# A decoder layer on one Trainium2 core: stick-breaking attention ahead of the banded attention, its branch merged second, and plain gates in the merge for the DeltaNet branch alone

## The chip, the core and the metric

The kernel runs on one core of one Trainium2 chip. A core has five engines with a queue each: TensorE (PE, matmuls and transposes), VectorE (DVE), ScalarE (ACT), GpSimd (POOL) and SyncE (SP, which here issues DMAs). An engine takes its instructions in order; across engines they wait on semaphores. The metric is the device time of one execution in microseconds.

## The reference, cut to what matters

One layer of a hybrid decoder over 512 tokens of width 2048. The part that the change touches is the mixer: three branches on the same input, each multiplied by its own sigmoid gate and summed.

```python
def hybrid_mixer(xn, w_in, ..., w_br_dn, w_br_swa, w_br_sb, w_o):
    proj = xn @ w_in
    ...
    o_dn = gated_delta_rule(q, k, v, g, beta)
    ...
    y_swa = sliding_window_gqa(...)      # banded: 8 heads of 64, window 128, ALiBi, sinks
    y_sb = stick_breaking_attention(...) # 4 heads of 128
    gate = jax.nn.sigmoid(gates).reshape(bsz, seq, N_BRANCH, D_MODEL)
    merged = gate[:, :, 0] * (y_dn @ w_br_dn) + gate[:, :, 1] * (y_swa @ w_br_swa) + gate[:, :, 2] * (y_sb @ w_br_sb)
    return merged @ w_o
```

Before it stands an RMSNorm; behind it follow a cross-attention, a convolutional FFN and a last norm, which the change leaves alone.

## The kernel before

All activations lie transposed: a tile is 128 channels by 512 tokens. Products keep float32 accuracy by splitting each operand into a rounded part (`h`, `wh`) and a remainder (`l`, `wl`); three matmuls replace one. `dense` (lines 151 to 170) computes a 128 x 512 output tile so: it loads 512 KB of weights at a time into `raw` (three buffers), ACT casts them to `wh` (line 163), DVE forms `wl` (line 164), each with two buffers used in the order in which the program asks for them, and PE runs three matmuls for each of 16 pieces of the inner dimension: 48 in all (lines 168 to 170).

The stages, in the program's order:

1. Input norm and transposes; `xh`, `xl` are the split input.
2. Gates. There are 16 column tiles (`m`) for each of three branches (0 DeltaNet, 1 banded, 2 stick-breaking). `strassen_pair` computes two of them in seven half-size products (56 pairs of a 512 wide and a 256 wide matmul; line 366 is the first of each). For `m` from `MP` = 2 on, all three branches' gates go this way, through the sigmoid and to DRAM; then the DeltaNet values (four more pairs).
3. DeltaNet (region `p_dn`).
4. Region `p_b`: the banded attention, then the stick-breaking attention.
5. Merge (region `p_c`): for each `m` and each branch, the gate (for `m` < 2 by `dense`, otherwise read from DRAM into `sg`), then the branch's product with its weights, then gate times product, summed into `mrg[m]`. At `m` = 0 the branch inputs `y` are split into `yh` and `yl`; these tiles lie in the region's memory, which the region before it used.
6. Output projection and the rest.

The banded attention projects K and V (one `dense` each), and then for each of four head pairs a Q tile. A pair's 512 queries go in four blocks. A block is a chain: scores on PE (line 750, two heads), bias on DVE (756), row maximum (760) and small operations, exponentials on ACT (765, 767), normalisation on DVE (769 to 771), transposes on PE (774), a copy on ACT (776), the product with the values on PE (779). The first block of a pair has 128 keys a head, the others 256. A stick-breaking head projects V, K and Q (three `dense` tiles), and then has one chain over all keys (lines 797 to 845).

Each engine's order is made when the program is built: a scheduler places each instruction by its priority and by when its operands and buffers are expected to be free. A weight load and its split have a raised priority. Dense matmuls of later tiles are so placed between the steps of a chain, as far as buffers for their weights and sums are to be had: `dense` sums have two PSUM buffers (`acc`), everything else in these stages six (`gps`). An engine never leaves the order made so.

The merge loop, and the order of its branches:

```python
for m in range(KT):
    for b, (w, k0, nk) in enumerate(((w_br_dn, 0, 8), (w_br_swa, 8, 4), (w_br_sb, 12, 4))):
        sg = misc.tile([P, S], F32, name="sg")
        if m < MP:
            acc = dense_ps()
            dense(acc, w_in, 0, KT, O_G + b * D + m * P, xh, xl)
            last = act.activation(sg, acc, AF.Sigmoid)
        else:
            nc.sync.dma_start(out=sg, in_=gate_d[b][m])
```

Of the kernel before, what the change touches and what calls it, by code (L numbers as in the profile page):

```python
# [9 lines left out]
F32 = mybir.dt.float32  # L10
# [3 lines left out]
AF = mybir.ActivationFunctionType  # L14
ALU = mybir.AluOpType
AX = mybir.AxisListType

P = 128
S = 512
D = 2048  # L20
KT = D // P
# [7 lines left out]
O_WQ, O_WK, O_WV = 4112, 4624, 4752  # L29
O_SQ, O_SK, O_SV, O_G = 4880, 5392, 5904, 6416  # L30
# [28 lines left out]
def decoder_kernel(ctx: ExitStack, tc: tile.TileContext, x, mem, norm_mix, w_in, dn_conv, dn_a_log, dn_dt_bias, dn_norm,  # L59
                   swa_sinks, w_br_dn, w_br_swa, w_br_sb, w_o, norm_xattn, norm_mem, w_xq, w_xkv, w_xo, norm_ffn, w_up,  # L60
                   ffn_conv, w_down, norm_final, consts, out, dbg=None):
    nc = tc.nc
    act, dve, pool, pe = nc.scalar, nc.vector, nc.gpsimd, nc.tensor
# [32 lines left out]
    def dense_ps():  # L96
        return psd.tile([P, S], F32, name="acc")

    def gen_ps():
        return gen[0].tile([P, S], F32, name="gps")  # L100
# [39 lines left out]
    def mrg_tile(k):  # L140
        return mrgp.tile([P, S], F32, name=f"mrg{k}")
# [9 lines left out]
    def dense(acc, w, r0, nk, col, hs, ls, M=P, share=False):  # L151
        for c0 in range(0, nk, 8):
            kc = min(8, nk - c0)
            raw = rawp.tile([P, 8, M], F32, name="raw")
            r = r0 + c0 * P
            with tc.high_priority(1000000):
                nc.sync.dma_start(out=raw[:, :kc, :], in_=w[r:r + kc * P, col:col + M].rearrange("(k p) c -> p k c", p=P))
            wh = wsp.tile([P, 8, M], F32R, name="wh")
            wl = wsp.tile([P, 8, M], F32R, name="wl")
            for s0 in range(0, kc, 4):  # L160
                part = slice(s0, s0 + 4)
                with tc.high_priority(1000000):
                    act.copy(wh[:, part, :], raw[:, part, :])  # L163
                    (pool if share and s0 else dve).tensor_tensor(wl[:, part, :], raw[:, part, :], wh[:, part, :].bitcast(F32),  # L164
                                                                  op=ALU.subtract)
                for j in range(s0, s0 + 4):
                    k = c0 + j
                    pe.matmul(acc, wh[:, j, :], hs[k], start=(k == 0), stop=False)  # L168
                    pe.matmul(acc, wh[:, j, :], ls[k], start=False, stop=False)  # L169
                    pe.matmul(acc, wl[:, j, :], hs[k], start=False, stop=(k == nk - 1))  # L170
# [18 lines left out]
    with region("p_start") as ps:  # L189
# [9 lines left out]
        pt = gen_ps()  # L199
# [137 lines left out]
    with tc.tile_pool(name="psw", bufs=2, space=bass.MemoryType.PSUM, reuse_waits="tile") as pw:  # L337
# [78 lines left out]
            act.copy(la, d[:, HT:S])  # L416
            fold(out[:, 0, HT:S], d[:, 0:HT], la)

        for m in range(MP, KT, 2):
            for b_ in range(3):  # L420
                g = gp.tile([P, 2, S], F32, name="g", bufs=1)
                strassen_pair(w_in, O_G + b_ * D + m * P, g, m == MP and b_ == 0)
                act.activation(g, g, AF.Sigmoid)
                gd = dram.tile([P, 2, S], F32, name=f"gate{b_}_{m}")
                pool.dma_start(out=gd, in_=g)
                gate_d[b_][m], gate_d[b_][m + 1] = gd[:, 0, :], gd[:, 1, :]
# [284 lines left out]
    with region("p_b") as bp:  # L711
# [9 lines left out]
        for g in range(2):  # L721
            for f in range(2):
                pool.memset(kp[g][f][64 - 64 * f:128 - 64 * f, :], 0.0)
        acc = dense_ps()
        dense(acc, w_in, 0, KT, O_WK, xh, xl)
        for g in range(2):
            for f in range(2):
                act.copy(kp[g][f][64 * f:64 * f + 64, :], acc[64 * g:64 * g + 64, :])
        acc = dense_ps()
        dense(acc, w_in, 0, KT, O_WV, xh, xl)  # L730
        vt = misc.tile([P, S], F32, name="m0")
        act.copy(vt, acc)
        pt = gen_ps()
        for t in range(4):
            pe.transpose(pt[:, t * P:(t + 1) * P], vt[:, t * P:(t + 1) * P], ident)
        wv = bp.tile([P, 4, P], F32, name="wv", bufs=1)
        dve.tensor_copy(wv, pt.rearrange("p (t c) -> p t c", t=4))
        for pr in range(4):
            acc = dense_ps()
            dense(acc, w_in, 0, KT, O_WQ + pr * P, xh, xl)  # L740
            qt = bp.tile([P, S], F32, name="wq")
            act.activation(qt, acc, AF.Copy, scale=0.125)
            g = pr // 2
            yps = gen_ps()
            for b in range(4):
                nk = 1 if b == 0 else 2
                w = nk * P
                sps = gen_ps()
                for f in range(2):
                    pe.matmul(sps[:, f * w:(f + 1) * w], qt[:, b * P:(b + 1) * P], kp[g][f][:, (b + 1) * P - w:(b + 1) * P],  # L750
                              start=True, stop=True)
                s = bp.tile([P, S], F32, name="ws")
                sv = s[:, 0:2 * w].rearrange("p (f c) -> p f c", f=2)
                for f in range(2):
                    hd = 2 * pr + f
                    dve.scalar_tensor_tensor(s[:, f * w:(f + 1) * w], dist[:, 2 * P - w:2 * P], -(2.0 ** -(hd + 1)),
                                             sps[:, f * w:(f + 1) * w], op0=ALU.mult, op1=ALU.add)
                st = bp.tile([P, 5, 2], F32, name="wst", bufs=3)
                nm, es, sm_, rr = (st[:, i, :] for i in range(4))
                dve.tensor_reduce(nm, sv, axis=AX.X, op=ALU.max)  # L760
                sk = sink[:, 2 * pr:2 * pr + 2]
                dve.tensor_tensor(nm, nm, sk, op=ALU.max)
                dve.tensor_tensor(es, sk, nm, op=ALU.subtract)
                dve.tensor_scalar(nm, nm, -1.0, None, op0=ALU.mult)
                act.activation(es, es, AF.Exp)
                for f in range(2):
                    act.activation(s[:, f * w:(f + 1) * w], s[:, f * w:(f + 1) * w], AF.Exp, bias=nm[:, f:f + 1],
                                   accum_out=sm_[:, f:f + 1])
                dve.tensor_tensor(rr, sm_, es, op=ALU.add)
                dve.reciprocal(rr, rr)  # L770
                dve.tensor_tensor(sv, sv, rr.unsqueeze(2).broadcast_to([P, 2, w]), op=ALU.mult)
                tps = gen_ps()
                for i in range(2 * nk):
                    pe.transpose(tps[:, i * P:(i + 1) * P], s[:, i * P:(i + 1) * P], ident)
                pT = bp.tile([P, S], F32, name="wpT")
                act.copy(pT[:, 0:2 * w], tps[:, 0:2 * w])
                for f in range(2):
                    for i in range(nk):
                        pe.matmul(yps[64 * f:64 * f + 64, b * P:(b + 1) * P], wv[:, b + 1 - nk + i, 64 * g:64 * g + 64],
                                  pT[:, (f * nk + i) * P:(f * nk + i + 1) * P], start=(i == 0), stop=(i == nk - 1))  # L780
            y[8 + pr] = mrg_tile(8 + pr)
            act.copy(y[8 + pr], yps)
            dbg(f"y{8 + pr}", y[8 + pr])

        wid = [S - n * P for n in range(4)]
        off = [0, 512, 896, 1152]
        for h in range(4):
# [57 lines left out]
            act.copy(y[12 + h], ops)  # L845
            dbg(f"y{12 + h}", y[12 + h])


    mrg = [None] * KT
    with region("p_c") as cp:  # L850
        yh, yl = [None] * 16, [None] * 16
        for m in range(KT):
            for b, (w, k0, nk) in enumerate(((w_br_dn, 0, 8), (w_br_swa, 8, 4), (w_br_sb, 12, 4))):
                sg = misc.tile([P, S], F32, name="sg")
                if m < MP:
                    acc = dense_ps()
                    dense(acc, w_in, 0, KT, O_G + b * D + m * P, xh, xl)
                    last = act.activation(sg, acc, AF.Sigmoid)
                else:
                    nc.sync.dma_start(out=sg, in_=gate_d[b][m])  # L860
                if m == 0:
                    for k in range(k0, k0 + nk):
                        yh[k] = cp.tile([P, S], F32R, name=f"yh{k}", bufs=1)
                        yl[k] = cp.tile([P, S], F32R, name=f"yl{k}", bufs=1)
                        split(yh[k], yl[k], y[k])
                acc = gen_ps()
                dense(acc, w, 0, nk, m * P, yh[k0:k0 + nk], yl[k0:k0 + nk])
                if b == 0:
                    mrg[m] = mrg_tile(m)
                    dve.tensor_tensor(mrg[m], acc, sg, op=ALU.mult)  # L870
                else:
                    t = misc.tile([P, S], F32, name="m0")
                    dve.tensor_tensor(t, acc, sg, op=ALU.mult)
                    pool.tensor_tensor(mrg[m], mrg[m], t, op=ALU.add)
            dbg(f"mrg{m}", mrg[m])
# [372 lines left out]
```

## Time and profile before

| what | value |
|---|---|
| time, median of 3 runs | 2842.78 us (2842.43 to 2847.3) |
| the profiled execution's own time | 2845.59 us |
| its span, first to last instruction | 2843.8 us |
| its mean granted TensorE clock | 0.997 |
| gates and DeltaNet values in pairs | 129 to 629 us |
| banded attention | about 1034 to 1145 us |
| stick-breaking attention | about 1143 to 1281 us |

How to read it: a row of the timeline gives an instruction's start, its duration, engine, line of the kernel, operation and tiles (written from read); behind it, in brackets, how long the engine had been idle and what ended that. Matmuls are pipelined, so that the distance from one start to the next is shorter than a duration. A row of the groups or of a tile gives a count and durations in nanoseconds. In the windows view each engine has its busy time and its number of instructions in the stretch, then come the granted clock of TensorE (1.00 is full), the share of the DMA engines and the bandwidth.

### The profile page before, as it was taken

To read this page: it belongs to the slowest core of one execution; us is meant where nothing else is said; L and a number is where in the kernel's file an instruction comes from. 1 tells how busy PE (TensorE), PEld (TensorE's weight loads), DVE (VectorE), ACT (ScalarE), POOL (GpSimd) and SP (SyncE) were. 2 spreads that over 40 slices of the span, in tenths; PEclk is the share of its full clock that TensorE was granted. 3 is DMA by queue.
4 is the path that set the end of the run, shared out by engine and by line. 5 is a ranking of instruction groups with operands and counts; after the bars stand their busy time and mean duration, and the time that the engine had idled before them with its cause. 6 is when DMAs were issued, how large, how long until landed. Compare 5 with 4: busy or idle time off the path is not lost. (4 is left out here: it accounts for less than half of the span.)

```text
span 2843.8 us, 40775 instructions
## 1 busy us (share of the span) xinstructions
PE 2780.3 (98%) x15959; PEld 2404.1 (85%) x15959; DVE 1852.3 (65%) x2771; ACT 1258.3 (44%) x2099; POOL 349.6 (12%) x317
## 2 busy tenths in 40 slices
PE   7999999999999999999999999999999999999998
PEld 7788888888888877778888887789999999978886
DVE  7777787877777645334554345778888888743435
ACT  6455555545434434443323334645454545532223
POOL 3100000001011000010221111311111111100002
PEclk9999999999999999999999999999999999999999
DMA  6444444443122222223555433765656565553333
GB/s 211 135 134 138 136 133 127 134 127 93 56 69 59 54 69 70 66 70 91 160 170 167 137 116 92 227 163 136 151 136 152 135 152 135 170 163 124 120 97 112
DMA packets 528467, 354.53 MB, mean 125 GB/s; under 512 B 15345, under 2 KB 483810, under 8 KB 527634
## 3 DMA queue, kind: packets, MB, share of 16 engines
q1 hardware_dynamic: 487872, 303.74, 37.4%
q0 software_dynamic: 39760, 47.93, 7.6%
q8 instruction: 125, 2.05, 0.3%
q14 instruction: 68, 0.56, 0.1%
q10 hardware_dynamic: 642, 0.26, 0.0%
HBM read 316.74 MB, written 35.13 MB: 124 GB/s over the span
## 5 line engine op out<-in xcount | busy, mean ns | idle before, releaser
L168 PE MATMUL acc<-x,wh 128*128 128x512 f32 x1152 | 456.0, 396 | 0.5 <-ACT wh L163 0.5
L164 DVE TENSOR_TENSOR wl<-raw,wh 128x512 fp32r<-128x512 f32 x394 | 287.6, 765 | 257.7 <-ACT wh L163 254.7
L169 PE MATMUL acc<-x,wh 128*128 128x512 f32 x1152 | 455.4, 395 | 0.0
L170 PE MATMUL acc<-x,wl 128*128 128x512 f32 x1152 | 455.1, 395 | 0.2 <-DVE wl L164 0.2
L163 ACT CAST wh<-raw 128x512 fp32r<-128x512 f32 x408 | 234.8, 618 | 414.7 <-PE acc L169 212.8
L170 PEld LDWEIGHTS acc<-x,wl 128*128 128x128 f32 x1152 | 217.0, 188 | 45.7 <-issue 1.6
L168 PEld LDWEIGHTS acc<-x,wh 128*128 128x128 f32 x1152 | 217.0, 188 | 44.6 <-issue 1.2
L169 PEld LDWEIGHTS acc<-x,wh 128*128 128x128 f32 x1152 | 217.2, 189 | 44.0 <-issue 2.0
L1165 DVE TENSOR_TENSOR wl<-raw,wh 128x512 fp32r<-128x512 f32 x112 | 72.4, 688 | 131.9 <-ACT wh L1164 131.9
L1030 ACT CAST wh<-sraw 128x1024 fp32r<-128x1024 f32 x87 | 91.3, 1049 | 150.0 <-PE sa L1035 97.1
L1164 ACT CAST wh<-raw 128x512 fp32r<-128x512 f32 x112 | 63.9, 618 | 178.5 <-PE gps L1171 172.2
L1030 ACT CAST wh<-raw 128x1024 fp32r<-128x1024 f32 x87 | 91.1, 1048 | 111.0 <-PE sd L1035 58.4
L1034 PE MATMUL sa<-x,wh 128*128 128x256 f32 x464 | 131.4, 283 | 0.0
L1035 PE MATMUL sb<-fb,wh 128*128 128x256 f32 x464 | 131.4, 283 | 0.0
L1036 PE MATMUL sb<-fb,wl 128*128 128x256 f32 x464 | 131.4, 283 | 0.0
L1034 PE MATMUL sb<-fb,wh 128*128 128x256 f32 x464 | 131.4, 283 | 0.0
L1035 PE MATMUL sa<-x,wh 128*128 128x256 f32 x464 | 131.4, 283 | 0.0
L1036 PE MATMUL sa<-x,wl 128*128 128x256 f32 x464 | 131.4, 283 | 0.0
L362 DVE TENSOR_TENSOR wl<-sm,wh 128x1024 fp32r<-128x1024 f32 x67 | 82.1, 1226 | 62.0 <-ACT wh L361 62.0
L1031 DVE TENSOR_TENSOR wl<-sraw,wh 128x1024 fp32r<-128x1024 f32 x87 | 106.3, 1222 | 19.0 <-ACT wh L1030 19.0
L1031 DVE TENSOR_TENSOR wl<-raw,wh 128x1024 fp32r<-128x1024 f32 x87 | 106.1, 1219 | 17.1 <-ACT wh L1030 17.1
L361 ACT CAST wh<-sm 128x1024 fp32r<-128x1024 f32 x67 | 70.3, 1050 | 84.9 <-PE sb L366 28.9
(584 smaller groups left out, 7601.7 us busy)
## 6 DMA issues: line engine op xcount, KB each, us to landing
raw<-in_w_in_dram SPq DMA_DIRECT2D x146, 512.0 KB, 3.8
raw<-in_w_up_dram SPq DMA_DIRECT2D x70, 512.0 KB, 5.0
raw<-in_w_down_dram SPq DMA_DIRECT2D x64, 512.0 KB, 3.7
sraw<-in_w_up_dram SPq DMA_DIRECT2D x58, 512.0 KB, 4.6
sraw<-in_w_in_dram SPq DMA_DIRECT2D x50, 512.0 KB, 3.8
raw<-in_w_o_dram SPq DMA_DIRECT2D x32, 512.0 KB, 4.0
raw<-in_w_up_dram POOLq DMA_DIRECT2D x29, 512.0 KB, 7.0
gate<-g POOLq DMA_DIRECT2D x21, 512.0 KB, 2.9
```

What stands on the lines that cost most here:

```text
L163: act.copy(wh[:, part, :], raw[:, part, :])
L164: (pool if share and s0 else dve).tensor_tensor(wl[:, part, :], raw[:, part, :], wh[:, part, :].bitcast(F32), op=ALU.subtract)
L168: pe.matmul(acc, wh[:, j, :], hs[k], start=(k == 0), stop=False)
L169: pe.matmul(acc, wh[:, j, :], ls[k], start=False, stop=False)
L170: pe.matmul(acc, wl[:, j, :], hs[k], start=False, stop=(k == nk - 1))
L362: dve.tensor_tensor(wl, w, wh.bitcast(F32), op=ALU.subtract)
L1030: act.copy(wh, w)
L1031: dve.tensor_tensor(wl, w, wh.bitcast(F32), op=ALU.subtract)
L1034: pe.matmul(acc, wh[:, k, :], m[:, 0, :], start=(first and k == 0), stop=False, skip_group_check=True)
L1035: pe.matmul(acc, wh[:, k, :], m[:, 1, :], start=False, stop=False, skip_group_check=True)
L1036: pe.matmul(acc, wl[:, k, :], m[:, 0, :], start=False, stop=(k == 7), skip_group_check=True)
L1165: dve.tensor_tensor(wl, raw[:, i, :], wh.bitcast(F32), op=ALU.subtract)
```

## The change

Three edits, with no new function:

- Stage 2 makes gate pairs from `m` = 0 on, but for the DeltaNet branch only from `m` = 2. That is 23 gate pairs instead of 21. The variant of the first pair (`straight`) goes to the pair `m` = 0, branch 1.
- In region `p_b` the code of the stick-breaking attention stands ahead of that of the banded attention. Nothing inside either changes.
- In the merge the order of branches is 0, 2, 1, and only branch 0 computes plain gates, for `m` = 0 and 1; the four others of these tiles are read from DRAM.

```diff
-        for m in range(MP, KT, 2):
+        for m in range(0, KT, 2):
             for b_ in range(3):
+                if m < MP and b_ == 0:
+                    continue
                 g = gp.tile([P, 2, S], F32, name="g", bufs=1)
-                strassen_pair(w_in, O_G + b_ * D + m * P, g, m == MP and b_ == 0)
+                strassen_pair(w_in, O_G + b_ * D + m * P, g, m == 0 and b_ == 1)
...
-        acc = dense_ps()
-        dense(acc, w_in, 0, KT, O_WK, xh, xl)
...
-            y[8 + pr] = mrg_tile(8 + pr)
-            act.copy(y[8 + pr], yps)
-            dbg(f"y{8 + pr}", y[8 + pr])
-
         wid = [S - n * P for n in range(4)]
         off = [0, 512, 896, 1152]
         for h in range(4):
...
+        acc = dense_ps()
+        dense(acc, w_in, 0, KT, O_WK, xh, xl)
...
+            y[8 + pr] = mrg_tile(8 + pr)
+            act.copy(y[8 + pr], yps)
+            dbg(f"y{8 + pr}", y[8 + pr])
...
-            for b, (w, k0, nk) in enumerate(((w_br_dn, 0, 8), (w_br_swa, 8, 4), (w_br_sb, 12, 4))):
+            for b, w, k0, nk in ((0, w_br_dn, 0, 8), (2, w_br_sb, 12, 4), (1, w_br_swa, 8, 4)):
                 sg = misc.tile([P, S], F32, name="sg")
-                if m < MP:
+                if m < MP and b == 0:
```

In the changed kernel the lines of the banded attention are 65 higher (scores 815 instead of 750, transposes 839 instead of 774, product with the values 844 instead of 779), those of the stick-breaking attention 59 lower, and those of the merge 2 higher.

How the instructions stand. First PE before, in the middle of the banded attention's last pair; `ws` are the probabilities, `kp` and `wq` keys and queries, `acc<-x` a dense tile, here of the stick-breaking attention's projections.

```order
L168 MATMUL acc<-x_588,wh 128x512
L169 MATMUL acc<-x_588,wh 128x512
L774 MATMUL gps<-ident,ws 128x128 x4
L750 MATMUL gps<-kp_8945,wq 128x256
L750 MATMUL gps<-kp_8946,wq 128x256
L779 MATMUL gps<-wpT,wv 64x128 x4
L170 MATMUL acc<-x_588,wl 128x512
L168 MATMUL acc<-x_596,wh 128x512
L169 MATMUL acc<-x_596,wh 128x512
L170 MATMUL acc<-x_596,wl 128x512
L168 MATMUL acc<-x_604,wh 128x512
L169 MATMUL acc<-x_604,wh 128x512
```

Behind the scores (L750) and the product of the block before (L779) stand 23 dense matmuls, of which the first six are shown, before the next transposes. Now PE in the changed kernel, from the last two matmuls of the plain gate of `m` = 0 on; it is in the second block of the third head pair:

```order
L815 MATMUL gps<-kp_9306,wq 128x256
L169 MATMUL acc<-x_676,wh 128x512
L170 MATMUL acc<-x_676,wl 128x512
L839 MATMUL gps<-ident,ws 128x128 x4
L815 MATMUL gps<-kp_9305,wq 128x256
L844 MATMUL gps<-wpT,wv 64x128 x4
L815 MATMUL gps<-kp_9306,wq 128x256
L839 MATMUL gps<-ident,ws 128x128 x4
L815 MATMUL gps<-kp_9305,wq 128x256
L844 MATMUL gps<-wpT,wv 64x128 x4
L815 MATMUL gps<-kp_9306,wq 128x256
L839 MATMUL gps<-ident,ws 128x128 x4
```

So it goes on to the end of the stage: seven groups of transposes (L839) with no dense matmul between them. In four of the seven steps the product L844 stands between the two halves of the next scores. What follows on PE is the first branch's product:

```order
L815 MATMUL gps<-kp_9305,wq 128x256
L844 MATMUL gps<-wpT,wv 64x128 x4
L815 MATMUL gps<-kp_9306,wq 128x256
L839 MATMUL gps<-ident,ws 128x128 x4
L844 MATMUL gps<-wpT,wv 64x128 x4
L168 MATMUL gps<-yh_11313,wh 128x512
L169 MATMUL gps<-yl_11314,wh 128x512
L170 MATMUL gps<-yh_11313,wl 128x512
L168 MATMUL gps<-yh_11317,wh 128x512
```

The plain gate of `m` = 1 comes behind the branches of `m` = 0, but for its first eight matmuls, which stand ahead of the last few of the third branch. Last, ACT in the changed kernel around the sigmoid of the plain gate of `m` = 0 (L860); L830 and L832 are exponentials of a block, L841 the copy behind the transposes, L163 a weight cast:

```order
L832 ACTIVATE ws,wst<-ws,wst 128x128 x2
L841 COPY wpT<-gps 128x256
L163 CAST wh<-raw 128x512
L860 ACT_TABLE_LOAD
L860 ACTIVATE sg<-acc 128x512
L830 ACT_TABLE_LOAD
L830 ACTIVATE wst<-wst 128x2
L832 ACTIVATE ws,wst<-ws,wst 128x256 x2
L841 COPY wpT<-gps 128x512
```

Before, the first plain gate's sigmoid stood behind the last exponentials of the stage, with one table load ahead of it and none before the next plain gate's; now a table load stands on either side of it, inside the banded attention.

More of the change, by code (lines that the diff above doesn't have):

```diff
@@ L723, in decoder_kernel @@
                 pool.memset(kp[g][f][64 - 64 * f:128 - 64 * f, :], 0.0)
-        acc = dense_ps()
-        dense(acc, w_in, 0, KT, O_WK, xh, xl)
[L726 to L780, printed above, removed]
-            y[8 + pr] = mrg_tile(8 + pr)
-            act.copy(y[8 + pr], yps)
-            dbg(f"y{8 + pr}", y[8 + pr])
@@ L846, in decoder_kernel @@
             dbg(f"y{12 + h}", y[12 + h])
+        acc = dense_ps()
+        dense(acc, w_in, 0, KT, O_WK, xh, xl)
+        for g in range(2):
+            for f in range(2):
+                act.copy(kp[g][f][64 * f:64 * f + 64, :], acc[64 * g:64 * g + 64, :])
+        acc = dense_ps()
+        dense(acc, w_in, 0, KT, O_WV, xh, xl)
+        vt = misc.tile([P, S], F32, name="m0")
+        act.copy(vt, acc)
+        pt = gen_ps()
+        for t in range(4):
+            pe.transpose(pt[:, t * P:(t + 1) * P], vt[:, t * P:(t + 1) * P], ident)
@@ new lines, in decoder_kernel @@
+        wv = bp.tile([P, 4, P], F32, name="wv", bufs=1)
+        dve.tensor_copy(wv, pt.rearrange("p (t c) -> p t c", t=4))
+        for pr in range(4):
+            acc = dense_ps()
+            dense(acc, w_in, 0, KT, O_WQ + pr * P, xh, xl)
+            qt = bp.tile([P, S], F32, name="wq")
+            act.activation(qt, acc, AF.Copy, scale=0.125)
+            g = pr // 2
+            yps = gen_ps()
+            for b in range(4):
+                nk = 1 if b == 0 else 2
+                w = nk * P
+                sps = gen_ps()
+                for f in range(2):
+                    pe.matmul(sps[:, f * w:(f + 1) * w], qt[:, b * P:(b + 1) * P], kp[g][f][:, (b + 1) * P - w:(b + 1) * P],
+                              start=True, stop=True)
+                s = bp.tile([P, S], F32, name="ws")
+                sv = s[:, 0:2 * w].rearrange("p (f c) -> p f c", f=2)
+                for f in range(2):
+                    hd = 2 * pr + f
+                    dve.scalar_tensor_tensor(s[:, f * w:(f + 1) * w], dist[:, 2 * P - w:2 * P], -(2.0 ** -(hd + 1)),
+                                             sps[:, f * w:(f + 1) * w], op0=ALU.mult, op1=ALU.add)
+                st = bp.tile([P, 5, 2], F32, name="wst", bufs=3)
+                nm, es, sm_, rr = (st[:, i, :] for i in range(4))
+                dve.tensor_reduce(nm, sv, axis=AX.X, op=ALU.max)
+                sk = sink[:, 2 * pr:2 * pr + 2]
+                dve.tensor_tensor(nm, nm, sk, op=ALU.max)
+                dve.tensor_tensor(es, sk, nm, op=ALU.subtract)
+                dve.tensor_scalar(nm, nm, -1.0, None, op0=ALU.mult)
+                act.activation(es, es, AF.Exp)
+                for f in range(2):
+                    act.activation(s[:, f * w:(f + 1) * w], s[:, f * w:(f + 1) * w], AF.Exp, bias=nm[:, f:f + 1],
+                                   accum_out=sm_[:, f:f + 1])
+                dve.tensor_tensor(rr, sm_, es, op=ALU.add)
+                dve.reciprocal(rr, rr)
+                dve.tensor_tensor(sv, sv, rr.unsqueeze(2).broadcast_to([P, 2, w]), op=ALU.mult)
+                tps = gen_ps()
+                for i in range(2 * nk):
+                    pe.transpose(tps[:, i * P:(i + 1) * P], s[:, i * P:(i + 1) * P], ident)
+                pT = bp.tile([P, S], F32, name="wpT")
+                act.copy(pT[:, 0:2 * w], tps[:, 0:2 * w])
+                for f in range(2):
+                    for i in range(nk):
+                        pe.matmul(yps[64 * f:64 * f + 64, b * P:(b + 1) * P], wv[:, b + 1 - nk + i, 64 * g:64 * g + 64],
+                                  pT[:, (f * nk + i) * P:(f * nk + i + 1) * P], start=(i == 0), stop=(i == nk - 1))
+            y[8 + pr] = mrg_tile(8 + pr)
+            act.copy(y[8 + pr], yps)
+            dbg(f"y{8 + pr}", y[8 + pr])
```

## The prediction

> **What bounds the kernel now.** I read the page's totals first, then the waits of TensorE, then the timeline around the pieces that the change moves.
>
> ```profile
> span 2843.8 us, 40775 instructions
> PE 2780.3 (98%) x15959; PEld 2404.1 (85%) x15959; DVE 1852.3 (65%) x2771; ACT 1258.3 (44%) x2099; POOL 349.6 (12%) x317
> ```
>
> TensorE (PE) is busy 98% of the span, and no other engine comes near. Busy time of pipelined matmuls overlaps, so I price PE by start-to-start distances. Two stages matter; their rows in the windows view (busy time of PE, PEld, DVE, ACT, POOL, then granted clock, DMA share, GB/s), two rows of the waits (total, times, longest) and one of the timeline:
>
> ```profile
> 1034.00:1150.00 116.00, 114.86 (x596) 87.47 (x596) 62.61 (x177) 52.04 (x141) 0.00 (x0) 1.00 0.26 69
> 1281.00:1356.00 75.00, 75.00 (x331) 61.78 (x331) 33.56 (x49) 28.25 (x51) 4.94 (x3) 1.00 0.30 86
> PE gps L774 <- DVE ws L771: 0.9, 5, 0.2
> PE gps L832 <- ACT scuh L145: 4.4, 4, 1.1
> 1276.67 0.50 PE L168 MATMUL acc<-x,wh 128*128 128x512 f32 x1 [0.48 <-ACT wh L163]
> ```
>
> The first window is the banded attention, the second the start of the merge. PE hardly waits in either: for the softmax (`ws`) 0.9 us in all, for a stick-breaking head 1.1 us each, and 0.48 us once for weights in the last of these heads. So PE's own work sets the time as long as the program gives it something to do beside the softmax chains. The price of the change is therefore (a) PE work added or removed, and (b) time in which PE's queue holds nothing but a chain.
>
> **Gates.** Before, 21 gate pairs and 4 V pairs run as Strassen pairs; the last of a pair's seven products is `sd<-x`.
>
> ```profile
> L366 PE MATMUL sa<-x,wh x272: 392/398/498, 129.2 to 617.3; 128*128 128x512 f32 x136
> L366 PE MATMUL sd<-x,wh x136: 395/398/404, 148.1 to 625.8; 128*128 128x512 f32 x136
> 1010.42 0.39 PE L168 MATMUL acc<-x,wh 128*128 128x512 f32 x1
> ...
> 1012.46 0.39 PE L168 MATMUL acc<-x,wh 128*128 128x512 f32 x1
> raw<-in_w_in_dram SPq DMA_DIRECT2D x146, 512.0 KB, 3.8
> ```
>
> 25 pairs take 129.2 to 625.8 us plus one last step, some 0.35: 497/25 = 19.9 us a pair. In a plain tile, nine matmuls lie between the two L168 rows: 2.04/9 = 0.227 us, and 48 of them make 10.9 us. The change adds two pairs (39.8 us) and removes four plain tiles (43.5 us): **-3.7 us** of PE work. Beside them run two more stores on POOL's queue and four more 256 KB gate loads on SP's; the stores have some 1000 us until they are read, and the merge already makes such loads for 14 of its 16 tiles, ahead of their use. I cost them at 0; with that cover gone it would be one landing, about the 3.8 us of the last row (a weight load of twice that size).
>
> **Order.** Stick-breaking in front: its PE rows are the same 4/31/4/10/38 dense matmuls between its steps as before, so 0 (bounds: 1.1 us a head either way). Its last head is now covered by the K, V and first Q projections of the banded attention. The banded attention comes last, and its chain needs cover of its own. One block of it, with DVE and ACT not interrupted, is this:
>
> ```profile
> 1081.71 0.63 PE L774 MATMUL gps<-ident,ws 128*128 128x128 f32 x4
> 1082.17 1.03 PE L750 MATMUL gps<-kp,wq 128*128 128x256 f32 x4
> 1082.43 0.58 ACT L776 COPY wpT<-gps 128x512 f32<-128x512 f32 x1 [2.17 <-PE gps L774]
> 1083.13 0.67 PE L779 MATMUL gps<-wpT,wv 128*64 128x128 f32 x8
> 1083.24 0.75 DVE L756 SCALAR_TENSOR_TENSOR ws<-dist,gps 128x256 f32<-128x256 f32 x2 [1.68 <-PE gps L750]
> 1084.03 0.69 DVE L760 TENSOR_REDUCE wst<-ws 128x2 f32<-128x512 f32 x1
> 1085.14 0.20 ACT L765 ACTIVATE wst<-wst 128x2 f32<-128x2 f32 x1 [1.30 <-DVE wst L763]
> 1085.40 0.51 ACT L767 ACTIVATE ws<-ws,wst 128x256 f32<-128x256 f32 x1
> 1086.53 0.16 DVE L769 TENSOR_TENSOR wst<-wst 128x2 f32<-128x2 f32 x1 [1.22 <-ACT ws L767]
> 1086.92 0.69 DVE L771 TENSOR_TENSOR ws<-ws,wst 128x512 f32<-128x512 f32 x1
> ...
> 1087.76 0.63 PE L774 MATMUL gps<-ident,ws 128*128 128x128 f32 x4
> 1088.23 0.61 PE L750 MATMUL gps<-kp,wq 128*128 128x128 f32 x4
> 1092.51 0.38 PE L774 MATMUL gps<-ident,ws 128*128 128x128 f32 x2
> 1093.52 0.44 PE L779 MATMUL gps<-wpT,wv 128*64 128x128 f32 x4
> ```
>
> Scores (L750) to transposes (L774) take 5.59 us, of which PE works 1; for the narrow first block of a head pair 4.28. In the order of the changed kernel the next block's scores stand behind the transposes of the block before, so the blocks cannot overlap; a block costs 0.46 + 5.59 = 6.05 us. In four of the last seven blocks the probabilities' matmul (L779, now L844) stands between the two halves of the next scores: it can start 1.42 us behind the transposes (1083.13 less 1081.71), takes 0.6, and the second half another 0.55, so the bias add of that half starts some 0.7 us later: 6.75.
>
> Before, 22 or so dense matmuls (5 us) stand in each gap. Now the projections of pairs 1 to 3 and the one plain gate of tile 0 are used up when the scores of the third pair's second block have been issued. The next gate tile stands behind the branches, and the branches behind the last `y`. **Seven blocks have no cover**, and behind each waiting transpose stand all of PE's branch and gate matmuls. By the rows, counted from those scores:
>
> - Block A: 5.59, and the gate's sigmoid now falls into it. A weight cast, a table load, the sigmoid and a second table load stand ahead of its exponentials on ACT:
>
> ```profile
> 1278.33 1.28 ACT L858 ACT_TABLE_LOAD   x1
> 1279.62 0.60 ACT L858 ACTIVATE sg<-acc 128x512 f32<-128x512 f32 x1
> ```
>
> The gate's last matmul ends at about 1.7; cast 0.5, loads and sigmoid 1.28 + 0.6 + 1.28 give 5.4 where the exponentials would start at 2.97 (1085.14 less 1082.17). So 8.0.
> - B, C, F, G: 6.75 each. D, narrow: 0.46 + 4.28 = 4.75. E: 1.38 behind D's transposes, then 5.59: 6.95. Last probabilities: 2.05. Sum **48.8 us at full clock**.
>
> **Merge.** The splits of all sixteen `y` into `yh`, `yl` now stand behind the last of these on ACT and DVE.
>
> ```profile
> 1281.02 0.59 ACT L845 COPY mrg<-gps 128x512 f32<-128x512 f32 x1 [0.80 <-PE gps L843]
> 1281.50 6.87 ACT L145 CAST yh<-mrg 128x512 fp32r<-128x512 f32 x13
> 1282.16 6.71 DVE L146 TENSOR_TENSOR yl<-mrg,yh 128x512 fp32r<-128x512 f32 x11 [4.21 <-ACT yh L145]
> ```
>
> Before, gate tiles filled this; now tile 0's gates 1 and 2 come from memory. The first `yl` starts 1.2 us behind the last matmul; sixteen at 0.61 (6.71/11), with three weight splits and two gate products among them, end at 14.2, and the last branch's matmuls at 15.5. PE's work there is 48 branch and 8 gate matmuls, 12.7 us.
>
> Of 48.8 + 15.5 = 64.3 us PE works 6 blocks of 2.0, one of 0.95, two dense matmuls and 12.7: 26.2. Lost: 38.1. Off that come 1.4 us that PE waited there before (0.9 by the row above; 0.5 in the last stick-breaking head), and the 3.7 of the gates: **+33.0 us at full clock**.
>
> **The clock.** PE now idles about 4.2 us in every block (bias add to transposes). The trace has two idle times of that size:
>
> ```profile
> 2500.00:2502.00 2.00, 0.00 (x0) 0.00 (x0) 1.92 (x4) 2.00 (x4) 0.00 (x0) 1.00 0.51 182
> 2502.00:2504.00 2.00, 1.95 (x9) 1.80 (x10) 0.00 (x0) 0.75 (x2) 0.00 (x0) 0.52 0.85 229
> 1808.00:1810.00 2.00, 0.00 (x0) 0.00 (x0) 1.57 (x3) 0.98 (x2) 1.42 (x2) 0.79 0.91 294
> 1814.00:1816.00 2.00, 2.00 (x6) 1.57 (x5) 0.99 (x2) 0.84 (x2) 0.00 (x0) 0.50 0.01 5
> 2496.13 1.03 PE L1147 MATMUL acc<-ident,sg 128*128 128x128 f32 x8
> 2502.05 1.07 PE L1147 MATMUL acc<-ident,sg 128*128 128x128 f32 x4 [2.60 <-DMA sg<-h]
> 1814.32 0.63 PE L169 MATMUL acc<-x,wh 128*128 128x512 f32 x1
> 1814.75 0.63 PE L170 MATMUL acc<-x,wl 128*128 128x512 f32 x1
> ```
>
> 2.6 us of idling were enough for the granted clock to fall to half in the first pair of rows; in the second it came back only some 5 us after work had resumed. At half clock four transposes take 1.07 instead of 0.6, and a dense step is 0.43 (1814.75 less 1814.32) instead of 0.227, 1.88 times. A split block then takes: transposes 0.44 later, so the probabilities start at 1.84 and end 1.13 later; second scores 1.03; bias add to transposes 5.59 - 1.82 + 0.43: 8.2 instead of 6.75. D becomes 5.5, E 8.5, the last step 3.0: 8.0 + 4 x 8.2 + 5.5 + 8.5 + 3.0 = 57.8. In the merge the cold start costs 0.7 more, 16.2. Lost: 74.0 - 26.2 = 47.8; with -1.4 and -3.7: **+42.7 us**. I take this one, since the clock fell to half in both of the trace's idle times over 2.5 us after the first matmul; +33.0 stays as the other end. [...]
>
> The profiled execution took 2845.59 us (span 2843.8 and 1.8 around it); +42.7 on it is 2888.3. It lies 2.8 above the median 2842.78 (2842.43 to 2847.3), and on the median it is **2885.5**.
>
> **The rivals.**
> - The clock stays full between blocks: +33.0, 2875.8. For it: each block does 2 us of work. [...] Chance 0.25.
> - Faster than before: the tail's waits go under the PE work still queued, and only the gates count: 2842.8 - 3.7 = 2839.1. It decides where the seven blocks lose under 0.5 us each. Against it: the chain's own instructions sum to 5.2 of its 5.59 us (PE 1.0, DVE 0.75 + 0.69 + 0.69 and five small ones of 0.16, ACT 0.2 and, from 1085.40 to the release of DVE at 1086.53, 1.1), and no dense row stands between them. Chance 0.03.
> - The change does little, because the blocks overlap two deep (`ws` has two buffers): DVE's 2.9 us a block (the same numbers) would set the pace, 7 x 2.9 less PE's 13 is 7 lost, with the merge's 2.8, -1.4 and -3.7 some +5, 2848. Against it: the rows in PE's order. Chance 0.05.
> - Worse: SP's queue holds the second gate load of tile 0 until its buffer is freed, with the next weights behind it; two landings of 3.8 us come on top: 2893. Chance 0.07. For it: in-order queue; against: those weights are needed 20 us later.
>
> **How the numbers follow.** Forecast 2885.5 with chance 0.6. The range 2868 to 2895 holds it, the full clock (with 8 us below it, about 1 us a block, for the hand-offs I could only see with other work around them) and the dear merge; the 0.08 of the two small cases and the ends of the others stay out. A change under 0.2% (5.7 us) is about what a measurement cannot tell from none. Faster 0.03, same 0.03, slower 0.94.
>
> **What would show it.** After: pairs of 19.9 us, 27 of them; some 48 to 58 us with PE mostly idle ahead of the merge, waits of PE `gps` L839 on DVE `ws` of some 4 us each, seven times; a table load ahead of the exponentials of block A; granted clock near 0.5 there; first branch matmuls spaced by DVE's `yl`. If the waits are 1 us or less, or dense matmuls stand among them, the sum is wrong; if the clock stays at 1.00, the first rival is right.

## The result: 40 us slower, lost in one place

| | before | after |
|---|---|---|
| median of 4 runs each | 2845.04 us | 2885.92 us |
| lowest to highest | 2842.43 to 2847.51 | 2881.07 to 2888.22 |
| the profiled execution | 2845.59 (span 2843.8) | 2885.6 (span 2883.8) |
| mean granted clock | 0.997 | 0.988 |

Ratio 1.0138, 95% interval 1.0126 to 1.015.

The page of the changed kernel, its totals and two of the rows in 40 slices (each digit is the busy share, or the clock, of a slice of 72 us in tenths):

```profile
span 2883.8 us, 40890 instructions
PE 2791.0 (97%) x15991; PEld 2412.6 (84%) x15991; DVE 1873.3 (65%) x2789; ACT 1271.6 (44%) x2107; POOL 350.2 (12%) x319
...
PE   7999999999999999995999999999999999999998
...
PEclk9999999999999999996999999999999999999999
```

One slice stands out, the 19th, at 1298 to 1370 us: PE is half busy and its clock is down to six tenths. No engine is full there; it is a wait, and PE's waits name it. First the row that answers to `L774 <- DVE ws` (0.9 us before), then a wait that before did not have:

```profile
PE gps L839 <- DVE ws L836: 31.9, 10, 6.1
PE gps L168 <- ACT yh L145: 1.2, 1, 1.2
```

The timeline of PE in that slice, from the last scores that still had a dense tile beside them to the first branch product:

```profile
1302.44 1.13 PE L815 MATMUL gps<-kp,wq 128*128 128x256 f32 x4
1303.22 0.58 PE L169 MATMUL acc<-x,wh 128*128 128x512 f32 x1
1303.64 0.40 PE L170 MATMUL acc<-x,wl 128*128 128x512 f32 x1
1310.13 1.09 PE L839 MATMUL gps<-ident,ws 128*128 128x128 f32 x4 [6.09 <-DVE ws L836]
1311.01 1.06 PE L815 MATMUL gps<-kp,wq 128*128 128x256 f32 x2
1312.00 1.13 PE L844 MATMUL gps<-wpT,wv 128*64 128x128 f32 x8
1313.06 0.84 PE L815 MATMUL gps<-kp,wq 128*128 128x256 f32 x2
1318.45 1.08 PE L839 MATMUL gps<-ident,ws 128*128 128x128 f32 x4 [4.56 <-DVE ws L836]
...
1327.16 1.09 PE L839 MATMUL gps<-ident,ws 128*128 128x128 f32 x4 [4.56 <-DVE ws L836]
...
1332.67 0.41 PE L839 MATMUL gps<-ident,ws 128*128 128x128 f32 x2 [2.51 <-DVE ws L836]
...
1340.54 1.09 PE L839 MATMUL gps<-ident,ws 128*128 128x128 f32 x4 [4.56 <-DVE ws L836]
...
1349.02 1.09 PE L839 MATMUL gps<-ident,ws 128*128 128x128 f32 x4 [4.55 <-DVE ws L836]
...
1357.73 1.09 PE L839 MATMUL gps<-ident,ws 128*128 128x128 f32 x4 [4.56 <-DVE ws L836]
1359.55 1.13 PE L844 MATMUL gps<-wpT,wv 128*64 128x128 f32 x8 [0.73 <-ACT wpT L841]
1361.89 0.80 PE L168 MATMUL gps<-yh,wh 128*128 128x512 f32 x1 [1.21 <-ACT yh L145]
```

Seven groups of transposes each wait for a whole softmax, and no dense matmul stands between. The same four transposes that took 0.60 to 0.63 us before take 1.09. ACT in the first of these waits, and then the windows of four stretches (the granted clock is the third number from the end):

```profile
1303.84 0.62 ACT L163 CAST wh<-raw 128x512 fp32r<-128x512 f32 x1 [1.99 <-PE acc L169]
1304.47 1.28 ACT L860 ACT_TABLE_LOAD   x1
1305.77 0.60 ACT L860 ACTIVATE sg<-acc 128x512 f32<-128x512 f32 x1
1306.38 1.28 ACT L830 ACT_TABLE_LOAD   x1
1307.67 0.20 ACT L830 ACTIVATE wst<-wst 128x2 f32<-128x2 f32 x1
```

```profile
1304.00:1310.00 6.00, 0.03 (x1) 0.00 (x0) 3.16 (x10) 4.80 (x9) 0.00 (x0) 0.71 0.33 87
1310.00:1361.00 51.00, 24.07 (x102) 15.28 (x102) 16.89 (x54) 12.08 (x39) 0.00 (x0) 0.60 0.00 1
1361.00:1368.00 7.00, 6.11 (x14) 4.51 (x15) 6.13 (x11) 7.00 (x14) 0.00 (x0) 0.50 0.00 0
1368.00:1378.00 10.00, 9.57 (x42) 7.38 (x40) 7.62 (x11) 3.41 (x7) 1.61 (x1) 1.00 0.36 105
```

The plain gate's sigmoid puts two table loads, 1.28 us each, ahead of the first bare block's exponentials. The clock falls to half in that block and stays there until 1368, into the merge, but for three short returns (0.60 in the mean over the second window; the last section has them).

How much is lost can be measured between two marks that are the same in every kernel here: the last transposes of the DeltaNet stage (`ident,kd`) and the first of the output projection (`ident,xs`). Before, then after:

```profile
L692 PE MATMUL gps<-ident,kd x32: 271/273/332, 767.9 to 1015.2; 128*128 128x128 f32 x32
L919 PE MATMUL gps<-ident,xs x64: 270/272/273, 1518.8 to 1689.6; 128*128 128x128 f32 x64
```

```profile
L694 PE MATMUL gps<-ident,kd x32: 270/272/329, 808.3 to 1055.3; 128*128 128x128 f32 x32
L921 PE MATMUL gps<-ident,xs x64: 270/272/273, 1562.1 to 1732.8; 128*128 128x128 f32 x64
```

Before 1518.8 - 1015.2 = 503.6 us with six plain gates in it; after 506.8 with two. Four plain tiles are 43.5 us, so 460.1 would have been left: **46.7 us lost here**. The four tiles are paid for at the front: the stretch up to the first mark is 40.1 us longer, for two gate pairs. So the changed kernel is 43.3 us behind at the second mark.

### The profile page after: what moved, and what is told of

Read it like the earlier page. It is cut to its first block, busy times and chain, and to the rows that moved or that the text cites. A ratio compares the mean times of both kernels' runs of the same rounds, so it can differ in the third digit from the quotient of the medians.

```text
span 2883.8 us, 40890 instructions
## 1 busy us (share of the span) xinstructions
PE 2791.0 (97%) x15991; PEld 2412.6 (84%) x15991; DVE 1873.3 (65%) x2789; ACT 1271.6 (44%) x2107; POOL 350.2 (12%) x319
## 5 line engine op out<-in xcount | busy, mean ns | idle before, releaser
L164 DVE TENSOR_TENSOR wl<-raw,wh 128x512 fp32r<-128x512 f32 x378 | 276.0, 766 | 255.8 <-ACT wh L163 252.8
L168 PE MATMUL acc<-x,wh 128*128 128x512 f32 x1088 | 431.0, 396 | 0.0
L170 PE MATMUL acc<-x,wl 128*128 128x512 f32 x1088 | 429.8, 395 | 0.0
L169 PE MATMUL acc<-x,wh 128*128 128x512 f32 x1088 | 429.6, 395 | 0.0
L163 ACT CAST wh<-raw 128x512 fp32r<-128x512 f32 x392 | 225.7, 618 | 404.9 <-PE acc L169 197.6
L170 PEld LDWEIGHTS acc<-x,wl 128*128 128x128 f32 x1088 | 205.0, 188 | 42.1 <-issue 1.4
L169 PEld LDWEIGHTS acc<-x,wh 128*128 128x128 f32 x1088 | 205.2, 189 | 41.3 <-issue 1.5
L168 PEld LDWEIGHTS acc<-x,wh 128*128 128x128 f32 x1088 | 205.1, 189 | 41.3 <-issue 1.2
L1167 DVE TENSOR_TENSOR wl<-raw,wh 128x512 fp32r<-128x512 f32 x112 | 72.4, 688 | 133.7 <-ACT wh L1166 133.6
L1166 ACT CAST wh<-raw 128x512 fp32r<-128x512 f32 x112 | 64.0, 618 | 180.4 <-PE gps L1173 174.0
L362 DVE TENSOR_TENSOR wl<-sm,wh 128x1024 fp32r<-128x1024 f32 x72 | 88.2, 1225 | 65.2 <-ACT wh L361 65.2
```

## The experiments

All but the last of the kernels below differ from the kernel before or after in one part. Each time stands beside its own ratio to the kernel before, measured in the same session on the same chip; the kernel before had medians of 2845.04 us beside after, 2844.28 us beside gates_only to pipe and 2846.52 us beside the last three. "Lost" is the stretch between the marks, less 503.6, plus 10.9 for each plain tile that the kernel lacks.

| kernel | time, us | ratio to before (95%) | stretch, us | plain tiles | lost, us |
|---|---|---|---|---|---|
| after | 2885.92 | 1.0138 (1.0126 to 1.015) | 506.8 | 2 | 46.7 |
| gates_only | 2849.86 | 1.0023 (1.0006 to 1.004) | 468.7 | 2 | 8.6 |
| order_only | 2877.52 | 1.0127 (1.01 to 1.0153) | 535.5 | 6 | 31.9 |
| filler | 2873.08 | 1.0112 (1.0085 to 1.0139) | 492.3 | 2 | 32.2 |
| pipe | 2843.92 | 1.0 (0.9984 to 1.0017) | 465.0 | 2 | 4.9 |
| no_plain | 2897.29 | 1.0176 (1.0161 to 1.0192) | 496.6 | 0 | 58.3 |
| gate2_only | 2842.27 | 0.9983 (0.9974 to 0.9993) | 481.8 | 4 | 0.0 |
| pipe_gate1 | 2841.07 | 0.9981 (0.9972 to 0.9991) | 480.4 | 4 | -1.4 |

**The gates without the order (gates_only).** The kernel before, with the new gate loop and the new condition in the merge.

```diff
-                if m < MP:
+                if m < MP and b == 0:
                     acc = dense_ps()
```

> The change's gates alone (two more Strassen pairs, plain gates only for the DeltaNet branch), with the banded attention first and the branches in the old order. Theory (uncovered banded chain makes the loss): the last stick-breaking head loses the second gate tile as cover, about 1.6 us of waiting, and the splits of y stand open, about 3 to 4.5 us; with -3.7 us of TensorE work that is 2844 to 2848 against 2845 before, no difference. Rival (the loss comes from the gates: stores, loads, or missing plain tiles in the merge): most of the 40 us, 2875 or more.

Measured 2849.86, a little above the forecast: 8.6 us lost for 3.7 saved. It is the same mechanism on the other attention. PE's timeline at the end of the last stick-breaking head:

```profile
1323.10 3.81 PE L845 MATMUL gps<-sz,svv 128*128 128x512 f32 x8 [4.97 <-ACT sz L842]
1328.11 0.50 PE L168 MATMUL gps<-yh,wh 128*128 128x512 f32 x1 [1.19 <-ACT yh L145]
```

I had put that wait at 1.6 us; it is 5.0, and the product behind it ran 3.81 us instead of the 2.42 of the heads before it. The gates do not make the 40 us, but even alone they are no gain: what they save on PE they take away as cover.

**The order without the gates (order_only).** The kernel after, with the old gate loop and all six plain gates.

```diff
-                if m < MP and b == 0:
+                if m < MP:
                     acc = dense_ps()
```

> The new order of the attentions and of the branches alone, with all six plain gates kept in the merge. Theory: the plain gate of the second branch in the order adds 48 dense matmuls of cover, so about five blocks of the banded attention instead of seven lack it; lost there about 29 us, 2 to 3 in the merge, none gained from gates: 2873 to 2878. Granted clock falls to half there as well. Rival (order costs nothing by itself): 2845.

Measured 2877.52, lost 31.9. PE waits for `ws` 21.0 us in all instead of 31.9, in five long waits instead of seven. The order alone makes most of the loss, and one plain tile more inside the attention takes two blocks out of it.

**Useless work in the gaps (filler).** 140 matmuls are added; their sum is read by nothing. In the built order they also push the plain gate of `m` = 0 back: its last matmuls now stand behind the last block, ahead of the merge, and its sigmoid with one table load stands behind the attention.

```diff
+        idle = dense_ps()
+        for i in range(140):
+            pe.matmul(idle, xh[i % KT][:, 0:P], xh[i % KT], start=(i == 0), stop=(i == 139))
```

> The changed kernel with 140 matmuls of 128x512 added behind the banded attention in the program, whose sum nothing reads (31.8 us of TensorE work); the order places them in the gaps of the uncovered chains, and the plain gate of tile 0 behind them, partly ahead of the splits. Theory with the clock (half clock stretches a block from 6.75 to 8.2 us): the blocks run at full clock with 6 to 7 us each, the granted clock stays at 1.00 there, and the time falls by 10 to 15 us to 2870 to 2876 although TensorE has 31.8 us more work. Rival 1 (the chain is bound by VectorE and ScalarE and the clock does not matter): 2884 to 2888. Rival 2 (added TensorE work adds time): 2917.

Measured 2873.08: with 31.8 us more work on PE the kernel is 13 us faster than after. The two were timed in different sessions, and the intervals of their ratios overlap (1.0085 to 1.0139 and 1.0126 to 1.015); but all four runs lie below all four of after, and between the marks the stretch is 14.5 us shorter. The window of that stretch and five of the transposes in it:

```profile
1302.00:1360.00 58.00, 57.93 (x297) 43.62 (x295) 30.99 (x83) 26.53 (x67) 0.00 (x0) 1.00 0.10 29
1315.53 0.63 PE L839 MATMUL gps<-ident,ws 128*128 128x128 f32 x4
1321.59 0.63 PE L839 MATMUL gps<-ident,ws 128*128 128x128 f32 x4
1326.33 0.38 PE L839 MATMUL gps<-ident,ws 128*128 128x128 f32 x2
1333.41 0.63 PE L839 MATMUL gps<-ident,ws 128*128 128x128 f32 x4
1339.46 0.63 PE L839 MATMUL gps<-ident,ws 128*128 128x128 f32 x4
```

Clock 1.00, a block every 6.06 us, the narrow one 4.74, the one behind it 7.08. The loss between the marks, 32.2, is the filler's own 31.8: with the gaps filled hardly anything else is lost, in the attention or in the merge. The split blocks ran in 6.06 instead of 8.3 to 8.7 us. How much of that difference is the clock and how much the order is not separated by a run of its own: the filler also moved the two halves of the scores together. Where the order is the same, 5.51 stands against 4.74 us for the narrow block and 7.87 against 7.08 for the one behind it. So it is out that the chain is DVE's or ACT's limit, independent of the clock.

**The chain two deep (pipe).** `front` is a block up to its normalised probabilities, `back` its transposes and product.

```diff
+        prev = None
+        for pr in range(4):
+            qt, yps = query(pr)
+            for b in range(4):
+                s = front(pr, b, qt)
+                if prev is not None:
+                    back(*prev)
+                prev = (pr, b, s, yps)
+        back(*prev)
```

> The changed kernel with the banded attention written two deep: scores and softmax of the next block stand ahead of the transposes of the block before. Theory (the loss is a serial chain without cover): two blocks share one chain's time, the projections and the gate cover all of them, and no block is left bare; the loss shrinks to the splits in the merge (about 3 us), with -3.7 us of gates: 2843 to 2850. Rival (VectorE or ScalarE bound the stage, or the loss sits elsewhere, in the merge or its loads): 2865 or more.

Measured 2843.92, 42 us below after with the same arithmetic: with two chains side by side the four dense tiles in the stage suffice, and no wait of PE for `ws` is left. What is lost still, 4.9 us, is in the merge; PE waits there once for `yh`, another 0.7 us for `yl`, and behind the first wait its matmuls stand 0.43 us apart up to 1325.4, against 0.23 from there on:

```profile
1319.38 0.80 PE L168 MATMUL gps<-yh,wh 128*128 128x512 f32 x1 [2.90 <-ACT yh L145]
```

**No plain gate at all (no_plain).** `MP` is 0, so all 24 pairs run in the gate stage. With the last plain sigmoid a preload of ACT's tables falls away that hung on it, behind the merge.

```diff
-    MP = 2
+    MP = 0
```

> The changed kernel with no plain gate at all: all 24 gate pairs run as Strassen pairs, nothing dense stands in the merge, and no sigmoid inside the banded attention. Theory: 48 dense matmuls less cover, so nine blocks are bare instead of seven; with the block times measured in the changed kernel (5.5 narrow, 7.9 and 8.5 to 8.7 wide) the bare stretch is about 70 us instead of 58, lost 9 us more; gates -1.9; 2889 to 2896. The first bare block, without the table loads, takes 5.6 to 6.0 us from scores to transposes instead of 7.7. Rival (fewer plain tiles are a gain by themselves, as TensorE's work falls): 2884.

Measured 2897.29, 11 us above after though PE has 1.9 us less to do; 58.3 lost. The direction is as expected and the size a little larger. The first bare block missed its forecast: scores 1299.21, transposes 1305.64; then 1306.24 to 1312.71, 6.4 and 6.5 us and not 5.6 to 6.0. The two have different reasons. The first still had dense matmuls beside it until 1303.4; here a weight cast stood between the two exponentials on ACT. In the second the scores took 1.92 us where those of the first took 1.03, and its transposes 1.04, near the 1.09 of the changed kernel at half clock; that its clock had fallen too is an estimate from these lengths:

```profile
1303.15 0.62 ACT L163 CAST wh<-raw 128x512 fp32r<-128x512 f32 x1
1306.24 1.92 PE L815 MATMUL gps<-kp,wq 128*128 128x256 f32 x4
1312.71 1.04 PE L839 MATMUL gps<-ident,ws 128*128 128x128 f32 x4 [3.50 <-DVE ws L836]
```

Block A with its table loads took 7.69, so a block without them was 1.2 us shorter, not the 2 that I had expected.

**One pair, old order (gate2_only).** The kernel before with a Strassen pair for the first two tiles of the stick-breaking branch alone.

```diff
+                if m < MP and b_ < 2:
+                    continue
...
-                if m < MP:
+                if m < MP and b < 2:
                     acc = dense_ps()
```

> The kernel before with one change: the first two gate tiles of the stick-breaking branch run as a Strassen pair, the other four stay plain. Theory: the two plain gates of tile 0 that are left cover the last stick-breaking head and the splits, so only the gates' TensorE work changes, -1.9 us: 0.999 to 1.000 of the time before. Rival (any plain gate taken from the merge uncovers something): 1.001 or more.

Measured 0.9983 (0.9974 to 0.9993): faster. Between the marks nothing is lost: 481.8 is 503.6 less two tiles of 10.9. Of the 0.17%, the gates' 1.9 us are 0.07%, which the interval just reaches; the rest I cannot tell from scatter between executions.

**The best of both (pipe_gate1).** The two-deep kernel with plain gates for branches 0 and 2 and a pair only for branch 1.

```diff
-                if m < MP and b_ == 0:
+                if m < MP and b_ != 1:
                     continue
...
-                if m < MP and b == 0:
+                if m < MP and b != 1:
                     acc = dense_ps()
```

> The two-deep banded attention behind the stick-breaking one, with plain gates in the merge for the DeltaNet and the stick-breaking branch and a Strassen pair only for the banded branch's first two tiles. Theory: the plain gate of the second branch in the order fills the splits, which cost the two-deep kernel 4.9 us between the end of the DeltaNet stage and the end of the merge; with 1.8 us more TensorE work for gates that is some 2 to 3 us below the two-deep kernel, 2840 to 2844, at or just under the kernel before. Rival (the 4.9 us lie elsewhere): 2845 to 2848.

Measured 2841.07, 0.9981 (0.9972 to 0.9991), faster than before and after; PE's wait for `yh` is gone. It does not differ measurably from gate2_only. That fits: between the marks both lose nothing against before, and both have the same 22 gate pairs and four plain tiles.

## Why the prediction was right

- **Gates, -3.7.** The end of the pairs moved from 626.0 to 666.4 us (start of the last step), 0.8 of it from before the stage: 39.6 for two pairs, against 39.8. Two plain tiles less made the stretch of gate2_only 21.8 us shorter: 10.9 each.
- **Seven bare blocks.** Forecast 57.8 us from the scores of block A to the end of the last product; measured 1302.44 to 1360.68, 58.2. Block by block, forecast and measured: A 8.0 and 7.69; B, C, F, G 8.2 and 8.32, 8.71, 8.48, 8.71; D 5.5 and 5.51; E 8.5 and 7.87; last 3.0 and 2.95. The misses of the blocks run from -0.6 to +0.5 and partly cancel. E was shorter because the clock had come back for a moment: it was at 1.00 from 1330.5 to 1333.5, and the two transposes at 1332.67 took 0.41 us, with 0.38 to 0.41 before.
- **The merge, 16.2.** Measured 18.2 (to 1378.88, where the matmul behind the last branch's last one starts), and the reason was only half right: I had let DVE's remainders (`yl`) set the pace. DVE finished eleven of them in 6.71 us from 1361.87, while PE needed until 1368 to get its clock back and ran behind them; so the first branch's matmuls were not spaced by `yl`, as the prediction's signs had it. Only the last remainder held PE up. It took 1.78 us instead of 0.69, beside an addition on POOL:

```profile
1376.10 1.61 POOL L876 TENSOR_TENSOR mrg<-mrg,m 128x512 f32<-128x512 f32 x1 [163.41 <-DVE m L875]
1376.47 1.78 DVE L146 TENSOR_TENSOR yl<-mrg,yh 128x512 fp32r<-128x512 f32 x1
1378.31 0.50 PE L169 MATMUL gps<-yl,wh 128*128 128x512 f32 x1 [0.74 <-DVE yl L146]
```

- **The clock.** 0.60 in the mean over the bare blocks, where the sum had taken half for all of the work of PE from the first wait on. The choice between +33.0 and +42.7 was the open one, and it came out for the reason given: gaps of this size, 4.56 us in most of the blocks, took the clock down. The rival with a full clock would have shown 0.6 us transposes and 6.75 us blocks.
- **The sum between the marks** was 47.8 - 1.4 = 46.4; measured 46.7. That they are so near is luck, for two misses cancel. Bare blocks and merge together took 76.4 us instead of 74.0; and the work of PE to be taken off, 26.2 in the sum, comes to 28.3 by the measured loss (76.4 - 1.4 - 46.7). The blocks were priced too low there, at 2.0 and 0.95 us. Before, 236 dense matmuls, nine wide and three narrow blocks took 79.0 us from 1052.15 to 1131.13; at 0.227 a matmul and with 0.9 of waits this leaves 24.5 for the blocks, where the prices give 20.9. That is 0.3 a block, or 2.1 for the seven.
- **The total, +42.7**, measured +40.0 between the two profiled executions and +40.9 between medians. The 2.7 us too much are not in any term: at the second mark the difference was 43.3. Behind the merge, from the last `sqacc` matmul to the first up-projection pair, where no instruction differs, before took 68.2 us and after 65.7; the seven other kernels took 65.6 to 68.3, so it varies between executions. By an estimate about 1 us of these 2.5 is the clock: after PE's wait for `sqacc` it was at half until 1816.0 before, 4.2 us past the start of that matmul, and until 1856.1 in after, 2.0 us past it. That the forecast 2885.5 lies 0.4 from the median is luck too: the median of before that it was built on rose by 2.3 with the fourth run.
- **Rivals.** That the blocks overlap or the change does little: 31.9 us of waits for `ws` say no. That SP's queue makes two landings late: no wait of PE for weights of that kind stands in the merge. That the tail goes under the queued work: refuted by the same row; pipe shows what it would take, two chains in flight.

## What to carry to other kernels

Work taken off the bounding engine is worth its time only where it was not also the cover of somebody's latency: ask of each dense tile which chain it stands beside, and read in the built order what is left between that chain's steps. The stage that comes last in a region needs its cover from the next region. What may come forward from there is in the built order; that the buffers (weights, sums, memory reuse) decide it is argued here, and no run changed them. If the cover runs short, interleave two chains before looking for more of it: that alone brought 42 us here.

## What I had not expected of the hardware

Work without use made the kernel faster, 2873.08 against 2885.92 us: with the gaps filled the clock stayed at 1.00, and the plain gate that it pushed back covered the splits.

The clock fell some 2.5 us after PE went idle (last matmul done at 1304.04), and it came back for 3.4 us at a time, three times in the middle of the bare stretch. Seven half-microsecond windows of the changed kernel hold these changes:

```profile
1306.50:1307.00 0.50, 0.00 (x0) 0.00 (x0) 0.00 (x0) 0.50 (x1) 0.00 (x0) 0.56 0.92 179
1313.00:1313.50 0.50, 0.50 (x3) 0.44 (x2) 0.00 (x0) 0.00 (x0) 0.00 (x0) 0.62 0.00 0
1316.50:1317.00 0.50, 0.00 (x0) 0.00 (x0) 0.00 (x0) 0.50 (x3) 0.00 (x0) 0.80 0.00 0
1330.00:1330.50 0.50, 0.17 (x2) 0.00 (x0) 0.41 (x3) 0.28 (x1) 0.00 (x0) 0.55 0.00 0
1333.50:1334.00 0.50, 0.46 (x5) 0.29 (x5) 0.00 (x0) 0.00 (x0) 0.00 (x0) 0.86 0.00 0
1344.00:1344.50 0.50, 0.47 (x2) 0.00 (x0) 0.00 (x0) 0.00 (x0) 0.00 (x0) 0.90 0.00 0
1347.50:1348.00 0.50, 0.00 (x0) 0.00 (x0) 0.17 (x2) 0.26 (x2) 0.00 (x0) 0.52 0.00 0
```

All other half-microsecond windows from 1303 to 1370 show 0.50 or 1.00, so the means of these seven put the changes at 1306.56 (down), 1313.38 (up), 1316.80 (down), 1330.45 (up), 1333.86 (down), 1344.10 (up) and 1347.52 (down); the last is at 1368.0 (up). Their distances are 1, 2, 3, 4 and 6 times 3.41 us. So in this stretch of this run the clock changed only at whole multiples of 3.41 us from one another, and not a set time after PE stopped or started. In the 3.41 us before each of the four falls PE had worked at most 0.9 us, and in those before each of the four rises at least 3.0 us; 2.7 us of work in the 3.41 us up to 1364.58 (1361.89 to 1364.58) did not bring a rise. A gap's length alone therefore did not say here what became of the clock: it fell 2.5 us into the gap of 6.09 us before 1310.13, fell 2.9 us into the gap of 4.56 before 1318.45, and rose in the gap of 2.51 before 1332.67.
